# Down projection of a SwiGLU block: the second pair's weights are split ahead of the last pair's u, the first pair's sample products fill the gap, and y's stores go out on two queues

## The chip, the cores and the metric

One core of a Trainium2 chip (trn2) runs the whole program. The metric is the device time of one execution in microseconds (us). Three timed runs of the kernel before gave 1252.75, 1247.94 and 1252.57 us, median 1252.57 us. One further execution was profiled; every row below is from it.

## The reference, cut to what matters

One inference step of a small hybrid decoder trunk with one layer: 1024 prompt tokens and 8 x 8 sample tokens of width 1024 go through a normalised input projection, a sliding-window attention beside a gated linear attention, an output projection with residual, and then

```
def swiglu(h, w_gate, w_up, w_down):
    u = jax.nn.silu(jnp.einsum('btd,df->btf', h, w_gate)) * jnp.einsum('btd,df->btf', h, w_up)
    return jnp.einsum('btf,fd->btd', u, w_down)
...
        x = x + swiglu(rms_norm(x, norm2[l]), w_gate[l], w_up[l], w_down[l])
...
        xs = xs + swiglu(rms_norm(xs, norm2[l]), w_gate[l], w_up[l], w_down[l])
```

The hidden width is 2816, that is 22 blocks of 128 columns. The prompt's result y_prompt (1024 x 1024) and the samples' result y_sample (64 x 1024) leave at the end, all in float32. The change touches only the last product, u times w_down, the end of the stage before it, and the stores of the two results.

## The kernel before, in words

**Numbers in two parts.** Every float32 operand of a large product is split into a high part (rounded, made by a cast on ACT) and a low part (source minus high, made by a subtraction on DVE). `split_into` (L1245 to L1247) does both; in the profile they are the line L1246 on ACT and the line L1247 on DVE. `mm3` (L105 to L107) then multiplies high by high, high by low and low by high: three matmuls for each product. `mm2` (L111, L112) needs two, because there both parts of the left side sit in one tile.

**Up stage.** The 22 blocks are worked in NP = 11 pairs. For each pair the gate and the up product are formed as a 2 x 2 block product with seven multiplications (Strassen's scheme, in Winograd's form), in the order ORDER = 1, 2, 6, 7, 5, 4, 3. Its weights are two tiles `raw_wg` or `raw_wu`; the right side, the normalised tokens in split form, lies in the pools `h2a` and `h2b`. `tail` (L1353) multiplies the two results into `u`, stores 32 sample columns of each quarter into DRAM (`usd`, L1358), splits combinations of the prompt's quarters into `uo` (pool `uo`, 3 buffers) and stores these to DRAM (`ud`, L1364), all stores on ACT's DMA queue. For the last pair it makes only four plain parts (`put(1)`, `put(5)`, `put(2)`, `put(4)`, L1368), since that pair is multiplied without the seven-product scheme.

**Down stage.** The 11 pairs are taken in chunks of two, (0, 1) to (8, 9), and pair 10 alone. `blocks_W` (L1379) loads two tiles `raw_wd` of 512 KB for each pair on SP's DMA queue (`load_raw`, L83) and makes four splits `hi_wd`, `lo_wd` for each: `put(1, 0, 0)` from the first raw tile, `put(2, 3, 1)` from the second, then four subtractions on POOL (L1397 to L1400) that turn the raw tiles into the scheme's combinations, then `put(5, 7, 0)`, which needs the first two of these, and `put(4, 6, 1)`, which needs all four. Here the four splits of pair 1 are called #1 to #4. A POOL subtraction overwrites a raw tile, so it must wait until the split that reads it is done.

For each of four row groups `tp` the seven products are formed in the order DOWN = 1, 2, 3, 7, 5, 6, 4, both pairs of a chunk into the same PSUM bank (pool `psd`, 8 banks), and the result is copied to `Y[tp]` by ACT and DVE in turn (L1545, L1547) or added to it by DVE (L1543). In the first chunk at tp 0 the order is another: all seven products of pair 0 first, then all seven of pair 1, each in a bank of its own, so that pair 1's weights may come later (L1530 to L1533). The tiles `u` are read back from DRAM by SP (`load_u`, L1451), the samples by `load_u8` (L1466), which also splits them (`u8hl`). `samples` (L1476) forms the products of the 64 sample tokens for a chunk's pairs in two banks, one for each half of the columns, and adds them up in `Y8`: in the first chunk after tp 2, in the others after tp 1.

**End.** For pair 10 each row group has four products; each is added to `y` (L1564) and the row block of 256 KB is stored at once on ACT's queue (L1565), 16 stores in all. After tp 0 the samples of pair 10 are formed, `Y8` is finished by a copy on ACT (L1493) and two additions on POOL (L1494, L1495), and y_sample is stored on ACT's queue (L1496).

**What sets the order.** Only PE's order is the program's own (a manual schedule for that engine). On ACT, DVE, POOL and SP a scheduler places each instruction when the program is built, by what it expects to be ready; every engine then runs its list strictly in that order. A DMA issue sits in its engine's list as well, and where it waits, everything behind it on that engine waits too. The pools `raw3` (one tile for every fourth raw load) and `w2` (six of ten split tiles) lie where `h2b` was, and open only after the up stage's tail.

Of the kernel before, what the change touches and what calls it, by code (L numbers as in the profile page):

```python
# [37 lines left out]
def hymba_step(ctx: ExitStack, tc: tile.TileContext, x_prompt, x_sample, cache_k, cache_v, state_gla, meta,  # L38
# [1206 lines left out]
    def split_into(hi, lo, src):  # L1245
        nc.scalar.copy(hi, src)  # L1246
        nc.vector.tensor_tensor(lo, src, hi.bitcast(F32), op=ALU.subtract)  # L1247
# [104 lines left out]

    def tail(p, cu, cg):  # L1353
# [12 lines left out]
        if p == NP - 1:  # L1366

            put(1, a11), put(5, a21), put(2, a12), put(4, a22)  # L1368
            return
# [8 lines left out]

    def blocks_W(pairs, plain=False):  # L1379
# [4 lines left out]
        def put(i, j, n):  # L1384
            for B, raw in zip(W, raws):
                hl = parts("wd")
                split_into(*hl, raw[n])
                for c, m in enumerate((i, j)):
                    B[m] = tuple(a[:, c * 512:c * 512 + 512] for a in hl)
# [15 lines left out]
    for p in range(NP):  # L1405
        if p:
            full(A, cg)
        A = blocks_A(w_up_v, p, "wu")
        for a in cg:
            nc.scalar.activation(a, a, AF.Silu)  # L1410
        cu = c_tiles(c2pool, "u")
        full(A, cu)
        now = cu, cg
        if p < NP - 1:
            cg = c_tiles(c1pool, "g")
            A = blocks_A(w_gate_v, p + 1, "wg")
        else:
            W = blocks_W((0,))
        tail(p, *now)
# [3 lines left out]
    for p in (uopool_, c2pool_, c1pool_, h2apool_, raw2_, h2bpool_):  # L1423
        p.__exit__(None, None, None)
    psd_ = tc.tile_pool(name="psd", bufs=8, space=PSUM, reuse_waits="tile")
    psd = psd_.__enter__()
    def last_pool(*a):
        p, pool = open_pool(*a)
        ctx.push(p)
        return pool  # L1430

    raw3 = last_pool("raw3", 1)
    rawpool[1] = raw3
    w2 = last_pool("w2", 6)
    wpool.append(w2)
    nsplit[0] = 4
# [39 lines left out]
    def samples(pairs, first, last):  # L1476
# [12 lines left out]
        if last:  # L1489
# [6 lines left out]
            nc.scalar.dma_start(ys, y8)  # L1496
# [27 lines left out]
    for c, pairs in enumerate(CHUNKS):  # L1524
        first, last = c == 0, c == len(CHUNKS) - 1
        W = W + blocks_W((1,)) if first else blocks_W(pairs)
        for tp in range(4):
            U = [load_u(p, tp) for p in pairs]
            if first and tp == 0:
                pss = {m: pd() for m in ORDER}  # L1530
                for i, (u, B) in enumerate(zip(U, W)):
                    for m in DOWN:
                        mm3(pss[m], u[m], B[m], i == 0, i == 1)  # L1533
            for j, m in enumerate(DOWN):
# [17 lines left out]
            if tp == (2 if first else 1):  # L1552
                samples(pairs, first, False)
# [3 lines left out]
    for tp in range(4):  # L1557
        u, y = load_plain(NP - 1, tp), Y[tp]
        B = W[0]
        for c, (a1, a2), (b1, b2) in ((2, (1, 2), (1, 2)), (4, (5, 4), (1, 2)), (3, (1, 2), (0, 3)), (5, (5, 4), (0, 3))):  # L1560
# [4 lines left out]
            nc.scalar.dma_start(yp[rows(2 * tp + (c > 3)), D2 if c in (3, 5) else D1], y[c])  # L1565
        if tp == 0:
            samples((NP - 1,), False, True)
# [31 lines left out]
```

## Time and profile before

| what | us |
|---|---|
| median of three runs | 1252.57 |
| lowest and highest run | 1247.94, 1252.75 |
| profiled execution, its time | 1251.81 |
| profiled execution, its span | 1250.0 |
| PE busy in the span | 1202.7 (96%) |
| DVE, ACT, POOL busy | 873.2, 514.7, 415.7 |
| mean granted TensorE clock | 0.985 |

The time of an execution is a little more than its span, 1251.81 against 1250.0 us. Times in rows count from the start of the span. The up stage ends and the down stage begins at about 999.5 us; the last product ends at about 1243.5 us. A matmul's shown duration is longer than its share of the engine, since matmuls are pipelined; what counts is from the start of one to the start of the next.

### The profile page before, as it was taken

Reading aid. Unit: us, or ns where it says so; the run is one execution under the profiler, and the core shown is the slowest. Engines: PE = TensorE matmul, PEld = TensorE weight load, DVE = VectorE, ACT = ScalarE, POOL = GpSimd, SP = SyncE. Lnnn points to the kernel's source line nnn. Section 1 sums busy time; section 2 is a strip of 40 time slices with the busy share of each in tenths; the row PEclk is TensorE's granted clock in tenths of the full one; section 3 lists DMA queues with packets and bytes.
Section 4 is the critical chain, followed back from the end, with each engine's and each line's share of the span. In section 5 each row is a group of like instructions: output and inputs, shape, how many; then the busy total and the mean of one; then the engine's idle time right before and its main releaser. Section 6 shows DMA issues by size and latency. Waiting matters only on the chain.

```text
span 1250.0 us, 23188 instructions
## 1 busy us (share of the span) xinstructions
PE 1202.7 (96%) x9190; PEld 1066.3 (85%) x9190; DVE 873.2 (70%) x1742; ACT 514.7 (41%) x933; POOL 415.7 (33%) x360
## 2 busy tenths in 40 slices
PE   6999899999999999899999999999999979999997
PEld 6877788778777778789999999999999958888886
DVE  6746987698679876756667656666666666667786
ACT  5634665566566454433234323333332344112200
POOL 6212202131211101215434443544354433334653
PEclk9998999999999999989999999999999999999999
DMA  6723423242323544314435434442544486576545
GB/s 186 237 79 92 121 69 94 54 123 86 101 69 100 165 170 154 116 51 137 128 113 170 154 97 143 154 146 85 180 137 127 147 311 260 211 268 253 213 182 177
DMA packets 145178, 183.17 MB, mean 147 GB/s; under 512 B 15675, under 2 KB 113374, under 8 KB 145054
## 3 DMA queue, kind: packets, MB, share of 16 engines
q1 hardware_dynamic: 95438, 130.83, 32.0%
q10 hardware_dynamic: 47792, 43.98, 10.9%
q0 software_dynamic: 1840, 6.88, 1.6%
q8 instruction: 72, 1.18, 0.4%
q14 instruction: 36, 0.29, 0.1%
HBM read 131.86 MB, written 50.86 MB: 146 GB/s over the span
## 4 chain that ended last, share of the span: by engine, by line
PE 52%; issue 20%; POOL 13%; DVE 8%; ACT 4%; DMA 2%; SPq 0%; POOLq 0%; ACTq 0%; DVEq 0%
PE pd L106 6%; PE pd L107 5%; PE pd L105 5%; PE pw L105 2%; PE pw L106 2%; PE pw L107 2%; POOL raw_wu L1267 2%; PE pf L107 2%; PE pf L105 1%; PE pf L106 1%; POOL raw_wg L1265 1%; ACT hi_wg L1246 1%; PE gv L105 1%; DVE uo L1247 1%; POOL raw_wg L1264 1%
## 5 line engine op out<-in xcount | busy, mean ns | idle before, releaser
L105 PE MATMUL pd<-hi_wd,u 128*128 128x512 f32 x312 | 122.7, 393 | 5.0 <-ACT hi_wd L1246 5.0
L106 PE MATMUL pd<-lo_wd,u 128*128 128x512 f32 x312 | 123.4, 396 | 1.5 <-DVE lo_wd L1247 1.5
L107 PE MATMUL pd<-hi_wd,u 128*128 128x512 f32 x312 | 122.5, 393 | 0.0
L1246 ACT CAST hi_wg<-raw_wg 128x1024 fp32r<-128x1024 f32 (+1 forms) x44 | 41.4, 942 | 139.5 <-PE pf L106 65.9
L1247 DVE TENSOR_TENSOR uo<-u,uo 128x512 fp32r<-128x512 f32 x74 | 77.7, 1056 | 25.4 <-ACT uo L1246 24.0
L1543 DVE TENSOR_TENSOR y<-y,pd 128x512 f32<-128x512 f32 x112 | 73.5, 682 | 27.1 <-PE pd L107 27.1
L1247 DVE TENSOR_TENSOR lo_wu<-raw_wu,hi_wu 128x1024 fp32r<-128x1024 f32 (+1 forms) x44 | 49.2, 1119 | 55.8 <-ACT hi_wu L1246 55.8
L1246 ACT CAST hi_wd<-raw_wd 128x1024 fp32r<-128x1024 f32 x42 | 43.0, 1051 | 97.6 <-PE pd L107 38.4
L1246 ACT CAST uo<-u 128x512 fp32r<-128x512 f32 x74 | 44.7, 620 | 80.1 <-POOL u L1371 39.4
L105 PEld LDWEIGHTS pd<-hi_wd,u 128*128 128x128 f32 x312 | 58.9, 189 | 19.2 <-ACT hi_wd L1246 5.9
L106 PEld LDWEIGHTS pd<-lo_wd,u 128*128 128x128 f32 x312 | 59.0, 189 | 15.3 <-DVE lo_wd L1247 2.8
L1264 POOL TENSOR_TENSOR raw_wg<-raw_wg 128x512 f32<-128x512 f32 x11 | 18.4, 1669 | 160.6 <-DVE lo_wg L1247 135.4
L107 PEld LDWEIGHTS pd<-hi_wd,u 128*128 128x128 f32 x312 | 59.0, 189 | 12.6
L1247 DVE TENSOR_TENSOR lo_wg<-raw_wg,hi_wg 128x1024 fp32r<-128x1024 f32 (+1 forms) x44 | 48.9, 1112 | 27.8 <-ACT hi_wg L1246 27.8
L1247 DVE TENSOR_TENSOR lo_wd<-raw_wd,hi_wd 128x1024 fp32r<-128x1024 f32 x42 | 61.1, 1466 | 7.8 <-ACT hi_wd L1246 7.7
L1246 ACT CAST hi_wu<-raw_wu 128x1024 fp32r<-128x1024 f32 (+1 forms) x44 | 41.3, 938 | 52.9 <-POOL raw_wu L1265 28.4
L590 POOL TENSOR_SCALAR sg<-sg 128x512 f32<-128x512 f32 (+1 forms) x9 | 14.1, 1564 | 133.9 <-ACT sg L589 133.9
L106 PE MATMUL pw<-lo_wo,hThi 128*128 128x512 f32 x128 | 51.2, 400 | 2.7 <-DVE lo_wo L100 2.7
L105 PE MATMUL pw<-hi_wo,hThi 128*128 128x512 f32 x128 | 52.2, 408 | 0.0
L107 PE MATMUL pw<-hi_wo,hTlo 128*128 128x512 f32 x128 | 50.9, 398 | 0.0
L1264 POOL TENSOR_TENSOR raw_wu<-raw_wu 128x512 f32<-128x512 f32 x11 | 14.2, 1291 | 91.6 <-DVE lo_wu L1247 91.6
L1410 ACT ACTIVATE g<-g 128x544 f32<-128x544 f32 x44 | 28.9, 657 | 22.8 <-DVE g L1300 18.9
(714 smaller groups left out, 4248.4 us busy)
## 6 DMA issues: line engine op xcount, KB each, us to landing
ud<-uo ACTq DMA_DIRECT2D x74, 512.0 KB, 4.4
u<-ud SPq DMA_DIRECT2D x40, 896.0 KB, 6.2
raw_wo<-in_w_o_dram SPq DMA_DIRECT2D x24, 512.0 KB, 3.8
raw_wu<-in_w_up_dram SPq DMA_DIRECT2D x22, 512.0 KB, 3.8
raw_wg<-in_w_gate_dram SPq DMA_DIRECT2D x22, 512.0 KB, 4.5
raw_wd<-in_w_down_dram SPq DMA_DIRECT2D x22, 512.0 KB, 4.1
raw_q<-in_w_in_dram SPq DMA_DIRECT2D x12, 512.0 KB, 5.0
raw_gv<-in_w_in_dram SPq DMA_DIRECT2D x12, 512.0 KB, 3.6
```

What stands on the lines that cost most here:

```text
L105: nc.tensor.matmul(ps, lh, rh, start=first, stop=False)
L106: nc.tensor.matmul(ps, lh, rl, start=False, stop=False)
L107: nc.tensor.matmul(ps, ll, rh, start=False, stop=last)
L590: nc.gpsimd.tensor_scalar(s, s, 2.0 ** 60, None, op0=ALU.min)
L1246: nc.scalar.copy(hi, src)
L1247: nc.vector.tensor_tensor(lo, src, hi.bitcast(F32), op=ALU.subtract)
L1264: nc.gpsimd.tensor_tensor(a22, a21, a22, op=ALU.add)
L1265: nc.gpsimd.tensor_tensor(a21, a11, a21, op=ALU.subtract)
L1267: nc.gpsimd.tensor_tensor(a12, a12, a11, op=ALU.subtract)
L1410: nc.scalar.activation(a, a, AF.Silu)
L1543: tt(a, a, ps, op=ALU.add)
```

## The change

Four edits. (1) The pools `raw3` and `w2` open before the last pair's `tail`, and pair 1's `blocks_W` is called there, so it stands before `tail` in the program. (2) In that `tail`, the DVE instructions of the four `put`s are queued behind `W_lo[5]`, the low part of pair 1's #2 (`W_lo` collects the low parts: 0 to 3 are pair 0's, 4 to 7 pair 1's). (3) At tp 0 of the first chunk the sample products of pair 0 are formed between pair 0's and pair 1's seven products, and those of pair 1 alone where both were formed before, after tp 2; so in this chunk `Y8` is first set by a copy and then added to. (4) The stores of y go out on POOL's queue for products 2 and 3 and on ACT's for 4 and 5; y_sample goes out on POOL's queue.

```diff
--- before.py
+++ after.py
@@ -1244,7 +1244,7 @@
 
     def split_into(hi, lo, src):
         nc.scalar.copy(hi, src)
-        nc.vector.tensor_tensor(lo, src, hi.bitcast(F32), op=ALU.subtract)
+        return nc.vector.tensor_tensor(lo, src, hi.bitcast(F32), op=ALU.subtract)
 
     def blocks_A(w, p, name):
 
@@ -1350,6 +1350,11 @@
         for m, ps in products(A, (0, 1), both):
             combine(t, slice(0, NH), m, ps[2])
 
+    def last_pool(*a):
+        p, pool = open_pool(*a)
+        ctx.push(p)
+        return pool
+
     def tail(p, cu, cg):
 
         tt, ts = nc.vector.tensor_tensor, nc.gpsimd.tensor_tensor
@@ -1365,7 +1370,8 @@
 
         if p == NP - 1:
 
-            put(1, a11), put(5, a21), put(2, a12), put(4, a22)
+            with tc.issue_after(W_lo[5].ins):
+                put(1, a11), put(5, a21), put(2, a12), put(4, a22)
             return
         put(1, a11), put(2, a12), put(4, a22)
         ts(a22, a21, a22, op=ALU.add)
@@ -1376,6 +1382,8 @@
         ts(a12, a12, a11, op=ALU.subtract)
         put(6, a11), put(3, a12)
 
+    W_lo = []
+
     def blocks_W(pairs, plain=False):
 
         W = [{} for p in pairs]
@@ -1384,7 +1392,7 @@
         def put(i, j, n):
             for B, raw in zip(W, raws):
                 hl = parts("wd")
-                split_into(*hl, raw[n])
+                W_lo.append(split_into(*hl, raw[n]))
                 for c, m in enumerate((i, j)):
                     B[m] = tuple(a[:, c * 512:c * 512 + 512] for a in hl)
 
@@ -1416,24 +1424,23 @@
             A = blocks_A(w_gate_v, p + 1, "wg")
         else:
             W = blocks_W((0,))
+
+            raw2_.__exit__(None, None, None)
+            h2bpool_.__exit__(None, None, None)
+            raw3 = last_pool("raw3", 1)
+            rawpool[1] = raw3
+            w2 = last_pool("w2", 6)
+            wpool.append(w2)
+            nsplit[0] = 4
+            W += blocks_W((1,))
         tail(p, *now)
 
 
     psp_.__exit__(None, None, None)
-    for p in (uopool_, c2pool_, c1pool_, h2apool_, raw2_, h2bpool_):
+    for p in (uopool_, c2pool_, c1pool_, h2apool_):
         p.__exit__(None, None, None)
     psd_ = tc.tile_pool(name="psd", bufs=8, space=PSUM, reuse_waits="tile")
     psd = psd_.__enter__()
-    def last_pool(*a):
-        p, pool = open_pool(*a)
-        ctx.push(p)
-        return pool
-
-    raw3 = last_pool("raw3", 1)
-    rawpool[1] = raw3
-    w2 = last_pool("w2", 6)
-    wpool.append(w2)
-    nsplit[0] = 4
     upool = last_pool("u", 4, "right")
     xpool2 = last_pool("x2", 2, "right")
     acc = last_pool("acc", 1, "right")
@@ -1473,7 +1480,7 @@
     def rows(t):
         return slice(t * P, t * P + P)
 
-    def samples(pairs, first, last):
+    def samples(pairs, first, last, W):
 
         US = [load_u8(p) for p in pairs]
         for half, blocks in ((D1, (1, 2)), (D2, (0, 3))):
@@ -1493,7 +1500,7 @@
             nc.scalar.copy(y8, Y8[64:128])
             ts(x8, x8, Y8[0:64], op=ALU.add)
             ts(y8, y8, x8, op=ALU.add)
-            nc.scalar.dma_start(ys, y8)
+            nc.gpsimd.dma_start(ys, y8)
 
     def residual(tp):
 
@@ -1523,7 +1530,8 @@
     CHUNKS = [(p, p + 1) for p in range(0, NP - 1, 2)]
     for c, pairs in enumerate(CHUNKS):
         first, last = c == 0, c == len(CHUNKS) - 1
-        W = W + blocks_W((1,)) if first else blocks_W(pairs)
+        if not first:
+            W = blocks_W(pairs)
         for tp in range(4):
             U = [load_u(p, tp) for p in pairs]
             if first and tp == 0:
@@ -1531,6 +1539,8 @@
                 for i, (u, B) in enumerate(zip(U, W)):
                     for m in DOWN:
                         mm3(pss[m], u[m], B[m], i == 0, i == 1)
+                    if i == 0:
+                        samples(pairs[0:1], True, False, W[0:1])
             for j, m in enumerate(DOWN):
                 if first and tp == 0:
                     ps = pss[m]
@@ -1550,7 +1560,7 @@
             if last:
                 combined(tp)
             if tp == (2 if first else 1):
-                samples(pairs, first, False)
+                samples(pairs[first:], False, False, W[first:])
 
 
     W = blocks_W((NP - 1,), True)
@@ -1562,9 +1572,9 @@
             mm3(ps, u[a1], B[b1], True, False)
             mm3(ps, u[a2], B[b2], False, True)
             tt(y[c], y[c], ps, op=ALU.add)
-            nc.scalar.dma_start(yp[rows(2 * tp + (c > 3)), D2 if c in (3, 5) else D1], y[c])
+            (nc.gpsimd if c in (2, 3) else nc.scalar).dma_start(yp[rows(2 * tp + (c > 3)), D2 if c in (3, 5) else D1], y[c])
         if tp == 0:
-            samples((NP - 1,), False, True)
+            samples((NP - 1,), False, True, W)
     psd_.__exit__(None, None, None)
 
 # ---- launch: one core; inputs and outputs as the reference has them ----
```

## Rows read from the trace of the kernel before

**Rows 1.** Stretches: length, busy us of the engines (instructions), granted clock, DMA share, GB/s.
```profile
1000.00:1010.00 10.00, 5.54 (x24) 3.84 (x22) 8.45 (x9) 4.57 (x7) 3.24 (x2) 1.00 0.99 334
1010.00:1020.00 10.00, 7.92 (x25) 5.67 (x26) 6.08 (x8) 4.33 (x8) 3.38 (x2) 0.83 0.78 258
...
1060.00:1210.00 150.00, 150.00 (x657) 123.09 (x656) 111.72 (x146) 27.20 (x31) 67.20 (x43) 1.00 0.62 234
```

**Rows 2.** Timeline of PE, 1004.5 to 1018.3: start, us, instruction, idle before and releaser.
```profile
1005.10 0.40 PE L107 MATMUL pd<-hi_wd,u 128*128 128x512 f32 x1
1009.95 0.50 PE L105 MATMUL pd<-hi_wd,u 128*128 128x512 f32 x1 [4.46 <-ACT hi_wd L1246]
...
1017.52 0.39 PE L107 MATMUL pd<-hi_wd,u 128*128 128x512 f32 x1
...
1018.22 0.39 PE L107 MATMUL pd<-hi_wd,u 128*128 128x512 f32 x1
```

**Rows 3.** Timeline of ACT and its DMA issues (ACTq), 984 to 1020.
```profile
999.75 2.00 ACT L1246 CAST hi_wd<-raw_wd 128x1024 fp32r<-128x1024 f32 x2 [2.03 <-PE pf L107]
...
1005.10 3.71 ACTq L1364 DMA_DIRECT2D ud<-uo  x3
1008.86 1.99 ACT L1246 CAST hi_wd<-raw_wd 128x1024 fp32r<-128x1024 f32 x2 [4.60 <-DVE uo L1247]
```

**Rows 4.** Timeline of DVE, 984 to 1020.
```profile
993.71 0.72 DVE L1299 TENSOR_TENSOR u<-u,pf 128x544 f32<-128x544 f32 x1 [2.31 <-PE pf L107]
...
998.50 2.31 DVE L1247 TENSOR_TENSOR lo_wd<-raw_wd,hi_wd 128x1024 fp32r<-128x1024 f32 x1
...
1002.11 2.35 DVE L1247 TENSOR_TENSOR lo_wd<-raw_wd,hi_wd 128x1024 fp32r<-128x1024 f32 x2
1004.38 4.03 DVE L1247 TENSOR_TENSOR uo<-u,uo 128x512 fp32r<-128x512 f32 x3
```

**Rows 5.** Timeline of POOL, 984 to 1020.
```profile
1004.55 1.65 POOL L1397 TENSOR_TENSOR raw_wd<-raw_wd 128x512 f32<-128x512 f32 x1 [4.83 <-DVE lo_wd L1247]
1006.28 1.59 POOL L1398 TENSOR_TENSOR raw_wd<-raw_wd 128x512 f32<-128x512 f32 x1
...
1013.51 1.28 POOL L1400 TENSOR_TENSOR raw_wd<-raw_wd 128x512 f32<-128x512 f32 x1
```

**Rows 6.** Timeline of SP's DMA queue (SPq), 984 to 1020.
```profile
992.64 0.42 SPq L83 DMA_DIRECT2D raw_wd<-in_w_down_dram  x1
998.31 6.84 SPq L1451 DMA_DIRECT2D u<-ud  x4
```

**Rows 7.** DMA issues of the whole run: queue, count, KB each, median us to landing.
```profile
ud<-uo ACTq DMA_DIRECT2D x74, 512.0 KB, 4.4
...
u<-usd SPq DMA_DIRECT2D x11, 64.0 KB, 6.9
```

**Rows 8.** Timeline of ACT, 950 to 1060: the copy of one half of the samples' sum.
```profile
1039.71 0.59 ACT L1486 COPY y<-pd 128x512 f32<-128x512 f32 x1 [1.24 <-PE pd L112]
```

**Rows 9.** Stretches at the end, columns as in the first group.
```profile
1236.00:1238.00 2.00, 2.00 (x10) 1.66 (x9) 1.35 (x3) 0.00 (x0) 2.00 (x1) 1.00 0.00 0
...
1246.00:1248.00 2.00, 0.00 (x0) 0.00 (x0) 0.00 (x0) 0.00 (x0) 0.00 (x0) 0.56 1.04 386
```

**Rows 10.** Timelines of POOL, ACT and DVE, 1215 to 1251: the end.
```profile
1235.67 2.40 POOL L1495 TENSOR_TENSOR y8lo<-y8lo,x 64x1024 f32<-64x1024 f32 x1
...
1238.10 0.54 ACTq L1496 DMA_DIRECT2D out_dram<-y8lo  x1
1238.74 7.66 ACTq L1565 DMA_DIRECT2D out_dram<-y  x11
...
1243.53 0.69 DVE L1564 TENSOR_TENSOR y<-y,pd 128x512 f32<-128x512 f32 x1 [0.68 <-PE pd L107]
```

**Rows 11.** DMA issues of the whole run, columns as in the seventh group.
```profile
x1d<-xr POOLq DMA_DIRECT2D x8, 512.0 KB, 3.9
...
out_dram<-y ACTq DMA_DIRECT2D x16, 256.0 KB, 3.3
```

## The prediction

> **What bounds the kernel now.** I read the split of the span into stretches first, to see where PE stands still, then the timelines of PE, ACT, DVE, POOL and SP around that place, and last the end of the run. In the stretches the reader sees PE at work without a break almost everywhere, as in the 150 us of the down stage from 1060 on; only from 1000 to 1020 is it busy 5.54 and 7.92 of 10 us, the second at a granted clock of 0.83 on the mean, partly at the lower of the levels of 1.2 and 2.4 GHz [rows 1]. So a change to this stage can win only what is lost there, and at the very end.
>
> **The loss in the gap.** A matmul of the down stage costs 0.23 us from start to start: 1017.52 to 1018.22 are three of them. The one at 1005.10 ends pair 0's products and the first of pair 1; the next could start at 1005.33. The rows at 1009.95 and 1017.52 are the first and the last of 15, so 14 were done between 1005.33 and 1017.52: 12.19 - 14 x 0.23 = 9.0 us lost, the slow clock counted in [rows 2].
>
> **Its cause.** ACT casts the high part of #1 by 1001.75, as second of a pair, and could go on with #2. But three stores of the last tail's u stand ahead of it in ACT's list, each waiting for its low part on DVE, where three took 4.03 us from 1004.38; the casts of #2 and #3 start at 1008.86, after 4.60 us of waiting [rows 3, 4]. PE waits 4.46 us for #2, and later for #4, which stands behind POOL's last subtraction, over at 1014.79 [rows 2, 5].
>
> **Edits 1 and 2, term by term.** Pair 1's splits come ahead of that u. I leave #1 where it is, since its cast now follows pair 0's last directly and I see nothing that makes it ready sooner: low part done at 1004.46 [rows 3, 4]. #2: its raw tile is issued on SP at 992.64 behind a load of u, and will now stand ahead of it [rows 6]; a cast takes 1.00 (half of 2.00), so its high part is there at about 1002.8, its low part after 1.18 us (half of 2.35), at 1005.6, or after 2.31 us where POOL works at the same time, at 1006.8 [rows 3, 4]. POOL's first two subtractions stay at 1004.55 to 1007.87; the third needs #2 and can follow at once. Two more at 1.28 to 1.65 end at 1010.5 to 1011.2 [rows 5]. #3 needs only the first two: cast from 1007.9, low part at 1010.2. #4: cast from 1010.6 to 1011.3, then 1.00 and 1.18: low part at 1012.8 to 1013.5. PE's sixth product waits for it at its second matmul; five matmuls, 1.15 us, remain, so pair 1 ends at 1014.0 to 1014.7.
>
> The u parts are then late: DVE's four come between or behind these splits, and their stores leave 5 us or more later. Who waits for that? Pair 10's products, the last of the stage, read them only after 1210, behind all of the 150 us of [rows 1]; what stands behind the stores on ACT is the copies of y, and PE has DVE's half of the banks meanwhile. I cost it at nothing here; if the cover goes, it is the last rival. On SP the raw load passed ahead of u's first load costs nothing as long as its buffer is free by then; if it is not, the u that PE needs at the start of the stage is late by at most the few tenths between the two issues plus one transfer, which I put at 1.5 us (512 KB at the 334 GB/s of that stretch [rows 1]) and keep for the range.
>
> **Edit 3.** Eight of the matmuls that now follow tp 2 move into the gap: 8 x 0.23 = 1.83 us that are no longer paid later. Seven of the eight banks are taken, so the second half must wait for the copy of the first: about 0.16 us to the end of its last matmul and 0.59 for the copy [rows 2, 8], 0.8 in all. Both lie before #3 is ready: products of pair 0 until 1004.64 (1005.33 less three), samples with that wait until 1007.3, three products until 1009.4, and #3's low part at 1010.2. What the load of the samples' u costs is not shown: it would be issued behind pair 1's u, after 998.31, and the median landing is 6.9 us, so 1005 or a little later, plus a small cast [rows 6, 7]. From below it is nothing, from above 2 us of waiting at the samples, and the first 1 to 2 of these are hidden under #3. I take nothing, as that wait ends before the one for #4. Two additions on DVE replace two copies on ACT for pair 1's half; PE is not held by either.
>
> Sum of the gap: without the change pair 1 ends at 1018.45 and eight sample products follow later, 1020.28; with it 1014.0 to 1014.7. That is 5.6 to 6.3 us; I take 5.9. A short wait may still cost the slow clock; the bound is what the clock of 0.83 lacks over its 10 us, 1.7 us [rows 1].
>
> **Edit 4.** At the end ACT's queue stands behind y_sample, which waits for POOL until 1238.07; the DMA engines' share is 0.00 from 1236 to 1238. Then 11 stores are issued in 7.66 us, 0.70 apart, the last at 1245.7, although its y is there at 1244.22; the transfers run at a share of 1.04 until after 1248 [rows 9, 10]. With y_sample and half of the stores on POOL's queue, each goes out when its y is ready, the last at about 1244.3: 1.4 us earlier. POOL's stores are not slower than that allows: 3.9 us to landing for 512 KB there, 3.3 for 256 KB on ACT [rows 11], and POOL's last y is there one product, 1.37 us, before ACT's. Waiting behind y_sample's additions on POOL delays only early stores. Bounds: nothing, if bytes alone set the end, and 2.4, if the last store also lands in 3.3 us instead of the 4.3 from its issue to the span's end at 1250.0. I take 1.4.
>
> The Trainium skill ("Trainium Kernel Development and Optimization", Key Constraints) speaks against this edit: DMAs of all queues run on the same 16 engines, and issuing from several saves only the issue time. The share of 1.04 agrees with it, the share of 0.00 before says that a blocked list costs more than issue time; by the rule alone the end would stay and the sum would be 5.9.
>
> **Sum.** 5.9 + 1.4 = 7.3 us off the profiled execution's 1251.8: 1244.5 us. That execution is 0.8 below the median of 1252.57. About 0.5%, 6.3 us, is what a measurement of this kernel can tell from no change.
>
> **The rivals.** (a) The whole gap closes, because #1 and #2 are done earlier: DVE has idle spells such as 2.31 us before 993.71 [rows 4], and its first raw tile is issued ahead of the one at 992.64. Then only the bank's 0.8 is left: 9.0 - 0.8 + 1.4 = 9.6, 1242.2 us. Against it: #1 did not use these spells before, though nothing in the rows held it.
>
> (b) The change does not do what it says: the scheduler sets ACT's and POOL's lists, the queueing binds only DVE's, and if the sample's cast or a load stands ahead of #2, PE waits as before. The gap is then merely filled: 1.83 + 1.4 = 3.2, 1248.6 us.
>
> (c) The transfers of the last stores bind the end: 1251.8 - 5.9 = 1245.9 us. For it speaks the share of 1.04 [rows 9].
>
> (d) Slower: u's ring of three buffers. Before, the first of the four parts was stored long before the others; now all four follow #2, so the fourth cast on ACT waits until the first store has landed. If that cast stands ahead of #3 in ACT's list, the chain is: #2 at 1006.8, the first part 1.34 (a third of 4.03), its issue, 4.4 us to landing [rows 3, 4, 7] or 6.9, as long as the slowest median: 1013 to 1016. Then the cast, its low part and its store, 2.5 us, two casts and a low part, 3.2, five matmuls and the slow clock, 2.9: pair 1 ends at 1021.6 to 1024.6 against 1020.28. Less the 1.4 of the end that is 1251.7 to 1254.7 us. It decides once #3's cast starts after about 1016. Against it: the program puts #3 ahead of that part.
>
> **How the numbers follow.** Forecast 0.48, with its own range 1243.3 to 1247; (a) 0.23; (b) 0.15; (c) 0.07; (d) 0.07. The range runs from (a) with the upper bound of the end and the scatter of the runs, 1240.5, to (b) with the same scatter, 1250.0, and leaves out (d) and what I have not seen. Faster by over 0.5% means under 1245.5: (a) and some seven tenths of the forecast, 0.23 + 0.34 = 0.57. Within 0.5%: the rest of the forecast, (b), (c) and most of (d), 0.40. Slower: 0.03, for (d) with more than one store waited for.
>
> **What would show it.** Right: ACT casts #2 directly behind #1, the three u stores come after it, PE's wait at the second product of pair 1 is gone, eight sample matmuls start at about 1004.6, and PE waits at most 1 us each for #3 and #4; the last store is issued by 1244.3 less the gap's gain. (a) is right if no wait for hi_wd or lo_wd is left. It is wrong if a wait of over 3 us stands between 1004 and 1016, for a u8 load, an uo store or a split, or if PE stands still after 1016 where it did not before.

## The result, and the profile after

Twenty runs of each on one chip: 1259.13 us median after, 1252.40 before, ratio 1.0053 with a 95% interval of 1.0040 to 1.0066. The change makes the kernel slower by about 6.7 us; 1244.5 was forecast, with a range up to 1250.0.

The profiled execution of the changed kernel took 1259.03 us, its span is 1257.3. Its down stage starts at 1001.75 us (before: 999.56). In the profiles below this start lies anywhere from 993.7 to 1001.8 (near 1040 in the two with a fourth buffer, part 3), also where the program up to there was not touched, so I count from it. The earliest goes with a mean granted clock of 0.990, the latest with 0.981. From the stage's first product to the last addition to y it was 244.66 us before; it is 250.42 after (1252.17 - 1001.75). From there to the span's end it was 5.78, and is 5.13. So the stage lost 5.76 and the end won 0.65: 5.1 us slower, the lower edge of what the interval allows (5.0 to 8.3).

The stretches of the changed kernel, columns as in [rows 1]:

```profile
1000.00:1010.00 10.00, 7.00 (x37) 5.36 (x35) 8.79 (x7) 4.10 (x5) 5.02 (x4) 1.00 0.85 316
1010.00:1020.00 10.00, 2.05 (x4) 1.17 (x4) 6.51 (x8) 3.75 (x6) 3.59 (x3) 0.52 0.91 319
```

The gap has become longer and has another shape: PE starts four matmuls between 1010 and 1020, and the granted clock falls to 0.52, that is to the lower level of 1.2 GHz, after PE has stood still. The timeline of PE there:

```profile
1006.60 0.40 PE L107 MATMUL pd<-hi_wd,u 128*128 128x512 f32 x1
1016.99 0.77 PE L111 MATMUL pd<-hi_wd,u8hl 128*128 128x512 f32 x1 [9.99 <-DVE u8hl L1247]
...
1020.94 0.79 PE L111 MATMUL pd<-hi_wd,u8hl 128*128 128x512 f32 x1 [1.91 <-ACT y L1493]
...
1024.33 0.39 PE L106 MATMUL pd<-lo_wd,u 128*128 128x512 f32 x1
```

The two waits in it are PE's only ones from 985 to 1060. Before, they were these (line, what it waited for, us in total, times, longest):

```profile
PE pd L105 <- ACT hi_wd L1246: 5.0, 2, 4.5
PE pd L106 <- DVE lo_wd L1247: 1.5, 2, 0.8
```

These waits for the splits of pair 1 are gone. In their place stands one of 9.99 us, for the split of the samples' u, and one of 1.91, for the copy that frees the bank of the second half. Counted as in [rows 2]: 12 matmuls start from 1006.83, where the next could have started, to 1024.33; 17.5 - 12 x 0.23 = 14.7 us lost, against 9.0. That is the 5.7 of the stage.

Why does an operation of 0.3 us come so late? The lists of the other engines (SP, DVE, POOL, ACT):

```profile
1000.88 0.42 SPq L1473 DMA_DIRECT2D u<-usd  x1
...
1006.92 2.17 DVE L1247 TENSOR_TENSOR lo_wd<-raw_wd,hi_wd 128x1024 fp32r<-128x1024 f32 x1 [0.26 <-ACT hi_wd L1246]
1011.31 1.32 DVE L1247 TENSOR_TENSOR lo_wd<-raw_wd,hi_wd 128x1024 fp32r<-128x1024 f32 x1 [2.23 <-ACT hi_wd L1246]
1012.55 2.95 DVE L1247 TENSOR_TENSOR uo<-u,uo 128x512 fp32r<-128x512 f32 x3
1015.43 1.21 DVE L1247 TENSOR_TENSOR lo_wd<-raw_wd,hi_wd 128x1024 fp32r<-128x1024 f32 x1
1016.56 0.28 DVE L1247 TENSOR_TENSOR u8hl<-u,u8hl 128x128 fp32r<-128x128 f32 x1
...
1006.74 1.26 POOL L1405 TENSOR_TENSOR raw_wd<-raw_wd 128x512 f32<-128x512 f32 x1 [4.82 <-DVE lo_wd L1247]
1008.08 2.12 POOL L1406 TENSOR_TENSOR raw_wd<-raw_wd 128x512 f32<-128x512 f32 x1
...
1005.84 1.05 ACT L1246 CAST hi_wd<-raw_wd 128x1024 fp32r<-128x1024 f32 x1
1010.24 1.04 ACT L1246 CAST hi_wd<-raw_wd 128x1024 fp32r<-128x1024 f32 x1 [3.35 <-POOL raw_wd L1406]
1011.19 0.29 ACT L1246 CAST u8hl<-u 128x128 fp32r<-128x128 f32 x1
1013.78 1.04 ACT L1246 CAST hi_wd<-raw_wd 128x1024 fp32r<-128x1024 f32 x1 [2.30 <-POOL raw_wd L1408]
1014.38 2.04 ACTq L1369 DMA_DIRECT2D ud<-uo  x3
1017.38 0.62 ACT L1246 CAST uo<-u 128x512 fp32r<-128x512 f32 x1 [2.55 <-DMA ud<-uo]
...
1020.31 0.58 ACT L1493 COPY y<-pd 128x512 f32<-128x512 f32 x1
```

Edits 1 and 2 did what they say: ACT casts #2 at 1005.84, #3 at 1010.24 and #4 at 1013.78, ahead of u's stores. But the samples' u, whose load was issued at 1000.88, is cast behind #3 (at 1011.19, without a wait for the load), and on DVE its low part stands behind #3's low part, three low parts of the last u, and #4's low part. When it ends at 1016.84, all of pair 1's weights are ready, and PE, whose list has the sample products first, could not take one of them. The copy of the first half then stands on ACT behind u's stores, behind a cast that waited 2.55 us for a buffer of u's ring, and behind a cast of the next chunk's weights.

The end: timelines of POOL, ACT and DVE.

```profile
1251.10 0.54 POOL L1575 DMA_DIRECT2D out_dram<-y  x1 [1.81 <-DVE y L1574]
...
1242.29 10.26 ACTq L1575 DMA_DIRECT2D out_dram<-y  x6
...
1251.48 0.69 DVE L1574 TENSOR_TENSOR y<-y,pd 128x512 f32<-128x512 f32 x1 [0.69 <-PE pd L107]
```

The last issue is over at 1252.55, 0.38 us after its y at 1252.17; in [rows 10] it was 2.18 after it (1246.40 against 1244.22). From there to the span's end it took 3.60 before and takes 4.75 now. 1.80 us earlier, 1.15 longer on the way: 0.65. The last stretches, before and after:

```profile
1248.00:1250.00 2.00, 0.00 (x0) 0.00 (x0) 0.00 (x0) 0.00 (x0) 0.00 (x0) 0.50 0.13 47
1254.00:1256.00 2.00, 0.00 (x0) 0.00 (x0) 0.00 (x0) 0.00 (x0) 0.00 (x0) 1.00 0.39 149
```

In stretches of 0.2 us, no transfer is left after 1248.4 before, 4.2 us after the last y, and after 1255.2 now, 3.0 us after it. So the transfers do end 1.2 us sooner; but the span runs on behind them for 2.1 us now and for 1.6 before, and no row shows what for.

### The profile page after: what moved, and what is told of

It is laid out like the page before. It is cut to its first block, busy times and chain, and to the rows that moved or that the text cites. A ratio compares the mean times of both kernels' runs of the same rounds, so it can differ in the third digit from the quotient of the medians.

```text
span 1257.3 us, 23187 instructions
## 1 busy us (share of the span) xinstructions
PE 1203.6 (96%) x9190; PEld 1067.8 (85%) x9190; DVE 874.6 (70%) x1744; ACT 515.0 (41%) x933; POOL 420.0 (33%) x369
## 4 chain that ended last, share of the span: by engine, by line
PE 51%; issue 21%; POOL 14%; DVE 8%; ACT 4%; DMA 1%; SPq 0%; POOLq 0%; ACTq 0%; DVEq 0%
PE pd L106 6%; PE pd L105 6%; PE pd L107 6%; PE pw L105 2%; PE pw L106 2%; PE pw L107 2%; POOL raw_wu L1267 2%; ACT hi_wg L1246 2%; POOL raw_wg L1265 1%; PE pf L107 1%; PE gv L105 1%; PE pf L105 1%; PE pf L106 1%; POOL raw_wg L1264 1%; PE gv L107 1%
## 5 line engine op out<-in xcount | busy, mean ns | idle before, releaser
L105 PEld LDWEIGHTS pd<-hi_wd,u 128*128 128x128 f32 x312 | 58.9, 189 | 13.2 <-issue 0.2
L106 PEld LDWEIGHTS pd<-lo_wd,u 128*128 128x128 f32 x312 | 58.7, 188 | 13.2 <-DVE lo_wd L1247 0.6
L1407 POOL TENSOR_TENSOR raw_wd<-raw_wd 128x512 f32<-128x512 f32 x10 | 16.4, 1643 | 66.6 <-DVE lo_wd L1247 66.5
```

The costliest lines, as they stand in the source:

```text
L105: nc.tensor.matmul(ps, lh, rh, start=first, stop=False)
L106: nc.tensor.matmul(ps, lh, rl, start=False, stop=False)
L1407: nc.gpsimd.tensor_tensor(b22, b22, b11, op=ALU.subtract)
```

## The experiments

**Theory A**, formed from this profile: PE goes through its list in order, so edit 3 lets pair 1's products wait for whatever the sample products wait for, and these wait for places in DVE's and ACT's lists. Edits 1 and 2 by themselves help. Rivals: edits 1 and 2 are the fault, by u's ring (rival (d) of the prediction); or sample products in the gap cost time by themselves. All kernels do the whole computation. Times in the text count from the span's start; "stage" is from the first down product to the end of the last addition to y.

**1. The parts alone.** The change without edit 3:

```diff
-                    if i == 0:
-                        samples(pairs[0:1], True, False, W[0:1])
...
-                samples(pairs[first:], False, False, W[first:])
+                samples(pairs, first, False, W)
```

> Edit 3 undone: edits 1, 2 and 4 stay, the sample products of both pairs follow tp 2 again. Theory A (the 10.0 us are the low part of the samples' u standing last in DVE's list, behind #3, three u parts and #4): with no sample product in the gap PE waits only for #2, #3 and #4. In the changed kernel their low parts were done at 1009.1, 1012.6 and 1016.6 with the stage starting 2.2 us later than before, so pair 1 ends at about 1017.8 against 1020.65 before: 2.9 us won, and 0.7 at the end by edit 4, about 1249 us, ratio 0.997. Rival B (splitting ahead of the last u is what costs, by contention on DVE and POOL): the gap stays over 9 us long and the time is 1252 us or more.

Measured 0.9989 (0.9974 to 1.0003), stage 242.70: 1.96 us shorter than before, where theory A had 2.9. PE's waits:

```profile
PE pd L106 <- DVE lo_wd L1247: 2.9, 3, 1.3
PE pd L105 <- ACT hi_wd L1246: 1.6, 2, 0.8
PE pd L105 <- ACT y L1555: 0.8, 1, 0.8
```

Edit 3 alone, on the kernel before:

```diff
+                    if i == 0:
+                        samples(pairs[0:1], True, False, W[0:1])
...
-                samples(pairs, first, False)
+                samples(pairs[first:], False, False, W[first:])
```

> The kernel before with edit 3 alone: pair 0's sample products between the two pairs' products, everything else as before. Theory A: the samples' split and the copy of their first half stand behind #2, #3 and #4 in the lists of ACT and DVE, so PE waits for the split until about 1012.5, then for the copy until about 1016.5, and pair 1's products come after: pair 1 ends at 1022 to 1024 against 1020.3 with the same work done before; 2 to 4 us slower, 1254 to 1256 us, ratio 1.002 to 1.003. Rival B (edit 3 is harmless, the earlier splits cost): the eight products fill the gap, 1.8 us faster, 1250.6 us.

Measured 1.0051 (1.0035 to 1.0068), stage 248.28. The wait for the split is about what theory A said, the one for the copy 0.7 us and not 4, and yet the time is worse than its 1.002 to 1.003. PE's two waits in the gap:

```profile
PE pd L111 <- DVE u8hl L1247: 8.8, 1, 8.8
PE pd L111 <- ACT y L1486: 0.7, 1, 0.7
```

Edit 4 alone:

```diff
-            nc.scalar.dma_start(ys, y8)
+            nc.gpsimd.dma_start(ys, y8)
...
-            nc.scalar.dma_start(yp[...], y[c])
+            (nc.gpsimd if c in (2, 3) else nc.scalar).dma_start(yp[...], y[c])
```

> The kernel before with edit 4 alone: y's stores on the queues of ACT and POOL, y_sample's on POOL's. From the last addition to y to the end of the span it took 5.8 us before and 5.1 in the changed kernel: about 0.7 us faster, 1251.7 us, ratio 0.9995, no difference that can be measured. As the prediction had it: 1.4 us faster, 1251.0. Rival C (POOL's queue costs at the end, or its DMA issues hold up POOL's additions): slower, 1253 us or more, and the last addition to y comes later than before, or the end more than 5.8 us after it.

Measured 0.9998 (0.9981 to 1.0015), stage 244.66 as before, end 5.11 instead of 5.78.

Edit 3 by itself makes the kernel slower by as much as the whole change, and without it the slowdown is gone: the fill is the cause, edits 1 and 2 are not. Without the fill PE waits five times for a split, 0.8 to 1.3 us each. Edit 4 gives 0.67 by the profile, too little for the runs to show. The runs put edit 3 at some 6 us, the profile at 3.6. In part that is the choice of executions: the profiled one of the kernel before took 1251.81 us, 2.0 more than the median of the runs beside edit 3 alone (1249.83), that of edit 3 alone 1254.82, 0.5 less than its own median (1255.34). An interval of 2.1 us to either side does not settle the rest.

**2. The waits of the fill taken away.** Pair 0's sample u loaded and split ahead of #1 to #4, in a pool of its own:

```diff
+            u80 = u8pool.tile([P, 2, 64], F32, tag="u80", name="u80")
+            nc.sync.dma_start(u80, usd[0].rearrange("p f a t -> p f (a t)"))
+            hl80 = u8pool.tile([P, 2, P], F32R, tag="hl80", name="hl80")
+            split_into(hl80[:, :, 0:64], hl80[:, :, 64:128], u80)
             W += blocks_W((1,))
```

> The changed kernel with pair 0's sample u loaded and split ahead of pair 1's splits, in a small pool of its own below the others. Theory A: the wait of 10.0 us at the first sample product goes. But the copy of the first half's sums still stands in ACT's list behind the three u stores, the fourth u cast, which waits for the first store to land, and two casts of the next chunk: PE waits there instead, for the second half, until about 1020, 9 to 11 us, and the time stays at 1256 to 1260 us. Rival D (the load itself lands late, the lists do not matter): with the load early nothing else is in the way, PE waits 1 us at most for the second half, pair 1 ends at about 1017.8 with the eight sample products done, 4.7 us won and 0.7 at the end: 1247 us.

Measured 1.0066 (1.0048 to 1.0084), stage 250.68. The wait for u8hl is gone and another has its place; PE and then ACT:

```profile
1021.11 0.80 PE L111 MATMUL pd<-hi_wd,hl 128*128 128x512 f32 x1 [13.12 <-ACT y L1498]
...
1017.51 0.62 ACT L1246 CAST uo<-u 128x512 fp32r<-128x512 f32 x1 [2.78 <-DMA ud<-uo]
...
1020.48 0.58 ACT L1498 COPY y<-pd 128x512 f32<-128x512 f32 x1
```

The samples' u is split in time (its cast is at 1005.71) and the first half is multiplied at once, but its copy runs at 1020.48, behind all casts, u's stores, the ring and a cast of the next chunk. PE waits 13.12 us for a bank, with seven others in use; theory A had 9 to 11. So the second wait was there all along, hidden behind the first.

The same with the first half alone in the gap, which needs no bank that a copy must free:

```diff
-                        samples(pairs[0:1], True, False, W[0:1])
+                        samples(pairs[0:1], True, False, W[0:1], ((D1, (1, 2)),))
...
+                    samples(pairs, True, False, W, ((D2, (0, 3)),))
+                    samples(pairs[1:], False, False, W[1:], ((D1, (1, 2)),))
```

> The changed kernel with pair 0's sample u loaded and split ahead of pair 1's four splits, and only the first half of its sample products (4 matmuls, 0.23 us each, into the eighth bank) in the gap; the second half comes later with the others, so no product needs a bank that a copy must free. Theory A (what cost time was that the fill waited, first for u8, then for the copy of its first half behind ScalarE's list): the matmuls of the gap wait for nothing, neither for u8hl nor for a copy; no wait of TensorE in the gap exceeds 1.5 us, the time is that of the version without the fill less up to 0.9, 0.997 to 0.999 of the kernel before. Theory B (sample products in the gap cost time by themselves, since they hold the eighth bank or lower the clock): the time stays above the kernel before, 1.003 or more.

Measured 0.9995 (0.9978 to 1.0013), stage 245.11. PE's waits:

```profile
PE pd L105 <- ACT hi_wd L1246: 1.5, 2, 0.8
PE pd L106 <- DVE lo_wd L1247: 1.3, 2, 0.8
PE pd L105 <- ACT y L1500: 1.2, 1, 1.2
```

The stretch from 1010 of the same run:

```profile
1010.00:1020.00 10.00, 6.16 (x14) 3.58 (x15) 7.88 (x9) 3.75 (x7) 3.01 (x2) 0.66 0.67 209
```

The same view of the version without a fill, whose gap lies 4.6 us earlier:

```profile
1000.00:1010.00 10.00, 6.29 (x23) 3.71 (x21) 7.48 (x7) 3.60 (x5) 6.87 (x4) 1.00 0.59 233
```

The fill itself waits for nothing, and the slowdown is gone: theory A's central claim is shown. Its size is not what theory A said: the waits are 4.0 us instead of 5.3, yet in the profile the stage is longer than without a fill, where the granted clock is 0.66 in that stretch and 0.83 in the next. But this is one execution of each: the one with the half fill took 1252.96 us, the second longest of its 12, the one without 1245.86, the third shortest of its 12. By the runs the two cannot be told apart (0.9995 and 0.9989, with intervals that overlap). So the fill did not cost waits and won nothing that the runs show; whether it lowers the clock, as theory B has it, stays open.

**3. The ring of u.** Four buffers instead of three, in the version with the samples' u early and both halves in the gap, and in the one without a fill:

```diff
-    uopool_, uopool = open_pool("uo", 3, "right")
+    uopool_, uopool = open_pool("uo", 4, "right")
```

> The version with pair 0's sample u early and both halves in the gap, with four buffers in u's output ring instead of three: the fourth cast of the last pair's u then waits for no store (2.78 us in the run with three). Theory A (the second half's wait is the copy's place in ScalarE's list, behind the fourth split's cast, u's stores and, in this list, no more the fourth cast): the wait of TensorE for the copy falls from 13.1 us by about 2.8 to 9 to 11 us and stays the longest of the gap; ratio 1.002 to 1.005. Rival (d) (the ring is what holds the copy): the wait falls to under 3 us and the time to 0.998 to 1.000.

> The version without the fill with four buffers in u's output ring instead of three. Theory A (without the fill no one on the path waits for the fourth cast of u): no change against the version without the fill, ratio 0.998 to 1.000, waits of TensorE within 1 us of it. Rival (the ring's wait of 2.5 us holds the copies that free pair 1's banks): the wait of 0.8 us for the first copy goes and the time falls by 0.8 to 2.5 us, 0.996 to 0.997.

Measured 1.0377 (1.0358 to 1.0396) and 1.0286 (1.0267 to 1.0305), neither near any expectation. The fourth buffer moves u's casts forward in ACT's list for all pairs, ahead of what the gate and up products wait for: in the changed kernel the copy of g (L1291) at 712.47 stands ahead of the last two of a pair's casts of u, with four buffers it runs at 727.33, behind all of them. PE's waits of the first over the whole span, where the kernel before has no group like the first line:

```profile
PE pf L105 <- ACT g L1291: 29.5, 10, 3.0
PE pd L111 <- ACT y L1498: 13.6, 1, 13.6
```

Its timeline of ACT in the gap, which lies about 40 us later:

```profile
1043.37 1.66 ACT L1246 CAST uo<-u 128x512 fp32r<-128x512 f32 x3 [0.84 <-DVE u L1362]
...
1059.71 0.59 ACT L1498 COPY y<-pd 128x512 f32<-128x512 f32 x1 [2.75 <-DMA ud<-uo]
```

So the totals tell nothing of the gap, but the gap can be read by itself. All of u's casts now run before #2, none waits for a buffer, and the copy still comes late; PE waits 13.6 us for it, where theory A said 9 to 11 and rival (d) under 3. So the ring's depth does not hold the copy. Its place behind u's stores does, and by the trace it waited 2.75 us more for one of these stores to land. That would fit a reuse of memory, as the down stage's pools open when the ring's is closed; this was not tried. In the version without a fill the wait of 0.8 for the first copy went, as the rival said, but the stage was no shorter (244.0 against 242.7; its granted clock was 0.61 from 1050 to 1060).

**4. u later still.** The last u behind #4 instead of #2, without a fill, and then the same with the later samples held behind the first copies:

```diff
-            with tc.issue_after(W_lo[5].ins):
+            with tc.issue_after(W_lo[7].ins):
...
+                    with tc.issue_after(first_copy[3].ins):
+                        samples(pairs, first, False, W)
```

> The version without the fill (edits 1, 2, 4) with the last pair's u held behind the fourth split instead of the third, so VectorE's list has all four low parts in a row. Theory A (with the fill gone, pair 1's splits end by GpSimd's four operations, 1.3 to 2.1 us each, and not by VectorE's list): the waits of TensorE for the splits stay within 1 us of the 5.8 us there, ratio 0.998 to 1.000. Rival (u's low parts in VectorE's list still hold the fourth split): the waits for the fourth split fall from 1.6 us to under 0.5 and the time by 1 to 2 us, 0.997.

> The version that held the last pair's u behind the fourth split (7.0 us of TensorE's wait for the first copy, 1.0046), with one thing more: the later sample products, and with them the two splits of sample u, are held behind the fourth of the first copies, so ScalarE's list has the copies ahead of them. Theory A (an engine goes through its list in order; the copies stood behind two small casts that waited 3.9 us for their load): the copies start as soon as u's last store is issued, the wait of 7.0 us falls to 0.8 to 3, the time to 0.999 to 1.002. Rival (d) (the ring of three buffers is what holds the copies: its fourth cast ran at 18.7, 5.2 us after the one before): the wait stays at 4 us or more, the time at 1.003 or more.

Measured 1.0046 (1.0029 to 1.0064) and 1.0019 (1.0004 to 1.0034). PE's longest wait in the first:

```profile
PE pd L105 <- ACT y L1555: 7.0, 1, 7.0
```

Its timeline of ACT:

```profile
1018.70 0.62 ACT L1246 CAST uo<-u 128x512 fp32r<-128x512 f32 x1 [5.15 <-DMA ud<-uo]
...
1023.24 0.30 ACT L1246 CAST u8hl<-u 128x128 fp32r<-128x128 f32 x1 [3.93 <-DMA u<-usd]
...
1023.98 0.58 ACT L1555 COPY y<-pd 128x512 f32<-128x512 f32 x1
```

The same wait in the second:

```profile
PE pd L105 <- ACT y L1556: 2.3, 1, 2.3
```

I expected no change from the first and got 5.8 us more than the kernel before, 7 more than the version without a fill; neither theory had this. The waits for splits stayed at 4.5 us (2.9 for low parts and 1.6 for high parts, as in part 1), as theory A said of them, so DVE's list does not set the splits' end. But the copies that free the first row group's banks now stood behind two casts of the samples' u that waited 3.93 us for their load. Putting the copies ahead of these took the wait from 7.0 to 2.3, as theory A expected, and the time to 1.0019. The 2.3 that remain lie behind u's fourth cast, which waits for the first store: there rival (d) is real, with a smaller price.

**5. POOL's chain.** Without the fill the splits end when POOL's four subtractions have ended, 1.3, 2.1, 1.3 and 2.1 us long, as in the changed kernel. There they hold up DVE and are held up by it: DVE's low part from 1006.92 takes 2.17 while POOL works until 1008.00, POOL's second then 2.12 while that low part runs until 1009.09; alone they take 1.2 and 1.3. The Trainium skill ("SBUF — State Buffer", Who interferes with whom) says that a DVE instruction with two SBUF inputs and a GpSimd instruction that reads SBUF share a port, and that the second to issue waits for the whole of the first; the rows agree. So pair 1's differences go to DVE (0.7 us each):

```diff
-    def blocks_W(pairs, plain=False):
+    def blocks_W(pairs, plain=False, eng=nc.gpsimd):
...
-            nc.gpsimd.tensor_tensor(b11, b12, b11, op=ALU.subtract)
+            eng.tensor_tensor(b11, b12, b11, op=ALU.subtract)
...
-            W += blocks_W((1,))
+            W += blocks_W((1,), eng=nc.vector)
```

with the later samples behind the copies as above, u behind #2 (`dve_late`) or behind #4 (`dve_hold4_late2`, which also holds the next pair's `blocks_W` behind the copies), and the first with the half fill of part 2 (`d1_dve_late`). Holding the samples by itself was not run; in the version without a fill the copies stood ahead of the samples' casts anyway (1013.88 and 1020.50).

> The version without the fill (edits 1, 2, 4), with pair 1's four differences on VectorE (0.7 us each) instead of GpSimd (1.3 to 2.1 us), and the later samples held behind the fourth copy as in the run beside it. Theory A (without the fill GpSimd's chain of 6.9 us ends the splits): the low part of the fourth split ends 1 to 2.5 us earlier than the 14.4 us after the down stage's start that it took there, the waits for splits fall from 4.5 to 2.5 to 3.5 us, and a part of it comes back as a wait for the first copy, since u's fourth cast still stands before it: ratio 0.997 to 0.999. Rival (the chain over the engines is bound by VectorE's own list, where u's low parts and the differences now stand): no gain or a loss, 0.999 to 1.001.

> The same with the last pair's u behind the fourth split, and the next weights' splits also held behind the fourth copy. Theory A: the splits end still earlier, about 12.4 us after the stage's start, but u's stores and the fourth cast come later and the copy behind them makes TensorE wait 2 to 4 us: what the splits gain is given back, ratio 0.998 to 1.000. Rival (the splits alone set the end of the gap): 0.995 to 0.997.

> The fastest version so far (edits 1, 2, 4 with the differences on VectorE and the later samples held back, 0.9968) with the first half of pair 0's sample products in the gap, split early, as in the run that had nothing to wait for there. Theory A (a fill that waits for nothing takes 4 x 0.23 = 0.9 us out of the gap's waits, but the eighth bank is then taken until a copy that stands behind u's last store, and TensorE waits for that copy where it waited 0.7 us): the waits for splits fall by up to 0.9, the wait for the first copy rises to 1.5 to 3 us; no gain from the fill, 0.996 to 0.999. Theory B (the fill pays once it waits for nothing): the copy's wait stays under 1 us, 0.995 to 0.996.

PE's waits of the first in the gap:

```profile
PE pd L106 <- DVE lo_wd L1247: 2.1, 2, 1.4
PE pd L105 <- ACT hi_wd L1246: 1.3, 1, 1.3
```

One more, for a copy on DVE, comes only 30.6 us after the stage's start:

```profile
1024.33 0.51 PE L105 MATMUL pd<-hi_wd,u 128*128 128x512 f32 x1 [0.74 <-DVE y L1554]
```

The stage starts at 993.74 here, so its gap lies in the stretch from 1000:

```profile
1000.00:1010.00 10.00, 6.55 (x25) 4.55 (x26) 8.83 (x13) 3.79 (x6) 0.00 (x0) 1.00 0.91 294
```

0.9968 (0.9951 to 0.9985), stage 241.41: the fastest version, clearly ahead of the kernel before and of the changed one. Its interval overlaps that of the version without a fill (0.9974 to 1.0003); what speaks for the move there is the profile: low part #4 ends 12.84 us after the stage's start (14.42 without it). With u behind #4 the ratio is 1.0000 (0.9982 to 1.0018): a wait for the first copy, behind the late u, takes back what the splits won:

```profile
PE pd L105 <- ACT y L1559: 3.5, 1, 3.5
```

With the half fill it is 0.9978 (0.9960 to 0.9996). PE's waits:

```profile
PE pd L105 <- ACT y L1500: 1.8, 1, 1.8
PE pd L105 <- ACT hi_wd L1246: 1.2, 1, 1.2
PE pd L106 <- DVE lo_wd L1247: 0.8, 1, 0.8
PE pd L111 <- DVE hl L1247: 0.6, 1, 0.6
```

Its stretch from 1010:

```profile
1010.00:1020.00 10.00, 7.41 (x19) 5.32 (x19) 4.08 (x7) 3.65 (x8) 0.00 (x0) 0.68 1.02 339
```

As theory A expected, a wait for the first copy comes, 1.8 us, since the half fill holds the eighth bank. Without the fill there is none in the gap: the 0.7 that the expectation names is the later wait for DVE. The waits are 4.4 us against 3.4; the rest of the stage's 2.7 goes with the clock. The intervals of the two versions overlap, so the runs show neither a gain nor a loss from the fill.

In the table the ratios are from all runs; waits and stage are from one profiled execution of each version, and executions of one version differ (the last one took from 1240.65 to 1252.54 us).

| version | ratio (interval) | PE's waits in the gap, us | stage, us |
|---|---|---|---|
| before | 1 | 6.5 | 244.7 |
| the change | 1.0053 (1.0040 to 1.0066) | 11.9 | 250.4 |
| edit 3 alone | 1.0051 (1.0035 to 1.0068) | 9.5 | 248.3 |
| change, samples' u early | 1.0066 (1.0048 to 1.0084) | 13.1 | 250.7 |
| the same, half a fill | 0.9995 (0.9978 to 1.0013) | 4.0 | 245.1 |
| change without edit 3 | 0.9989 (0.9974 to 1.0003) | 5.3 | 242.7 |
| without edit 3, u behind #4 | 1.0046 (1.0029 to 1.0064) | 11.5 | 250.4 |
| the same, samples behind the copies | 1.0019 (1.0004 to 1.0034) | 6.8 | 245.3 |
| without edit 3, samples behind the copies, differences on DVE | 0.9968 (0.9951 to 0.9985) | 3.4 | 241.4 |
| the same, u behind #4 | 1.0000 (0.9982 to 1.0018) | 6.4 | 244.6 |
| differences on DVE, half a fill | 0.9978 (0.9960 to 0.9996) | 4.4 | 244.1 |

## Why the prediction was wrong

**The step that failed** is in edit 3: of the samples' u, "I take nothing, as that wait ends before the one for #4". I had looked at when its load would land, 1005, and added "a small cast". The load was not the limit (its cast did not wait for it); the two operations of 0.3 us were, because their engines had #3, three parts of the last u and #4 ahead of them. Instead of nothing it was 9.99 us, five times my upper bound of 2. I had listed what the u parts delay on ACT and DVE, and never put the samples' split into the same lists, although the rule for that stands in the kernel's description: each engine goes through its list in order. The PE side of the same slip: I let the fill lie under the wait for #3, as if pair 1's products could start without it. They stand behind it in PE's list.

**The bank wait** of 0.8 us failed in the same way: matmul and copy by their durations, without the copy's place on ACT. It was 1.9 behind the first wait and 13.1 where that was gone. "PE has DVE's half of the banks meanwhile" was the cover I named for u's late stores; in the fill there is one free bank, and its copy is ACT's.

**Edits 1 and 2** were right in mechanism and too large: the wait of 4.46 us went, and no u store stood before the splits. #2 was not cast directly behind #1, as two casts of u (1004.79, 1.14 us) came between, but that made DVE wait only 0.26. Pair 1 should have ended 3.8 to 4.4 us earlier; without the fill it ended 15.75 us after the stage's start instead of 18.89, 3.1 earlier. Low part #4 came 14.4 us after that start, not 13.2 to 13.9: the prediction had POOL's last two subtractions at 1.28 to 1.65, while one of each two took 2.1. Behind pair 1 the prediction did not count the wait of 0.8 for the first copy, and the stage was only 2.0 shorter.

**Edit 4**: the issue came earlier by 1.8 us, somewhat more than the 1.4 of the text, but the way from the last issue to the end grew by 1.15, so 0.65 to 0.67 is what it gives. My bounds 0 and 2.4 held it. The transfers ended 1.2 us sooner after the last y, near the forecast; 0.5 went into the stretch behind them, which the prediction did not have. The DMA share is 1.02 from 1252 to 1254, so the row of rival (c) had some say. The Trainium skill ("Trainium Kernel Development and Optimization", Key Constraints) says that issuing from several engines saves only issue time, since all queues run on the same 16 DMA engines; the trace agrees in that the share is no higher with two queues than the 1.04 of [rows 9] with one.

**The rivals.** (b) came nearest in kind, "if the sample's cast or a load stands ahead of #2, PE waits as before"; what happened is its mirror image: the sample's split stood behind #4. (d) named the right list (ACT's), a ring wait that did come (2.55 us) and the right sign, but put it ahead of #3's cast, where it was not; it stood ahead of the copy. Its chance of 0.07, and 0.03 for slower, were far too small, since I had costed only the waits that the trace of before shows. The experiments say the fault was not in moving the splits.

**Open**: the part of the difference between 6 us in the runs and 3.6 in the profile of edit 3 alone that the choice of executions leaves; what the span waits for behind the last transfer; and what moves the granted clock, and with it the stage's start, from execution to execution.

## What to carry to other kernels

Work put into a gap of an in-order engine is a promise that its inputs are there: look up where each small operation that feeds it, and each copy that frees its bank, would stand in the lists of its own engines, and count everything that stands ahead, not only durations and landings. A filler that waits is worse than the gap, since the work behind it was ready; and when one wait is taken away, look for the next one behind it before counting the gain. Where two engines alternate on one chain and slow each other, as POOL and DVE here, moving the chain to one of them is worth a try before filling: here it gave the fastest version.

## What the runs showed that I had not expected

- **The clock after short waits.** With 5.3 us of waits in six pieces the clock stayed at 1.00 through the gap; with the half fill, 4.0 us of waits and PE busy 9.70 of the 10 us before, it fell to 0.66, and again to 0.68 in the last version with the half fill. It was after a standstill of 10 us that it fell to 0.52. Over all runs the mean clock points the same way, 0.984 with the half fill and 0.988 without, and 0.986 against 0.988 with the differences on DVE; but the place where it fell is known from one execution of each, and what decides is not shown here.
- **A fourth buffer cost some 37 to 39 us** (1.0377 against 1.0066, 1.0286 against 0.9989), by moving casts forward in ACT's list: 29.5 us of it are ten waits of some 3 us in the up stage, and the mean clock was lower too (0.972 against 0.983 in the first pair). A ring's depth is also an input to the scheduler.
- **Holding u behind one more split cost some 7 us** (0.9989 to 1.0046) without touching any operand of the gap: it moved two casts of 0.3 us ahead of the copies (putting the copies first brought it back to 1.0019), and u's fourth cast came later, for which PE still waited 2.3 us.
